# Start addresses of the float32r operand tiles moved onto multiples of 256 bytes

## The chip, the cores and the metric

The kernel runs on one core of one Trainium2 chip. The metric is the device time of one execution in microseconds (us), as the median of three runs. Beside the runs there is one profiled execution; all rows below come from it.

## What is computed

The reference is a decoder trunk of two layers over 256 tokens of width 1024, in float32.

```python
for i in range(2):
    h = rmsnorm(x, norm_mix[i]); memn = rmsnorm(mem, norm_mem[i])
    if i == 0: mix, q = s5_mixer(p[..., :768], ...), p[..., 768:]          # p = h @ w_in_a
    else:      mix, q = rwkv7_mixer(p[..., :2560], ...), p[..., 2560:]     # p = h @ w_in_b
    x = x + concat([mix, memory_cross_attn(q, memn, w_kv_mem[i])]) @ w_out[i]
    h2 = rmsnorm(x, norm_ffn[i])
    x = x + (swiglu(h2, ...) if i == 0 else moe_swiglu(h2, ...))           # dense, then 2 of 8 experts
return rmsnorm(x, norm_final)
```

Each of the 8 experts has a gate and an up matrix of 1024 x 3584 and a down matrix of 3584 x 1024.

## The kernel before

**Products.** Large products are made in float32r from operands split in two: a tile of weights `w` (2 MB, one DMA on SP's queue, `wload`, L63) is cut into 4 parts by `split` (L168 to 184). ScalarE writes the rounded part `wsh` (L182), VectorE the rest `wsl = w - wsh` (L183). Activations come as a pair as well (`xeh`/`xel`, `ath`/`atl`, `hTh`/`hTl`, `aTh`/`aTl`, `cath`/`catl`). `mm3` (L186) then issues three matmuls into one accumulator:

```python
TE.matmul(ps, xp[0], wh, ...)   # L188
TE.matmul(ps, xp[0], wl, ...)   # L189
TE.matmul(ps, xp[1], wh, ...)   # L190
```

The second argument is the operand that is loaded into the array (128 x 128, the row LDWEIGHTS of engine PEld); the third streams through it, 512 columns at a time. A profile row names the streaming operand first: `gu<-wsh,xeh`.

**Stages.** S5 mixer, memory attention and the first output projection (0 to 200 us), the dense SwiGLU ("FFN" below, to about 390 us), RWKV-7 (to 565 us), the second output projection and the router (to 615 us), and the expert layer (615 to 1615 us). The expert layer walks 8 experts x 7 chunks of 512 hidden columns, 56 jobs. A job has 24 matmuls for gate, 24 for up (both write `gu`, the loaded operand is `xe`) and 24 for down (accumulators `yac`, the loaded operand is `at`, the transposed activation of the job before), and four transposes against `ident` (L1646). Down matmuls of one job stand between gate and up matmuls of the next. Fetching an expert's tokens (`Gather`: `Gm` loaded, `xhp` streaming, L1448) comes in chunk 3 of the expert before; adding its result back (`combine`, L1681 and L1682) comes between gate and up of chunk 1 of the expert after. Weights pass through a ring of seven 2 MB tiles, the parts `wsh` and `wsl` through four buffers each.

**Addresses.** Tiles come from pools that are stacked in SBUF, some from the low end, some (`side="right"`) from the high end. `pad(pool, n)` takes n bytes. Even experts keep `Gm`, `xe`, `GT` and the small tile `wsl` of row weights (L1473; another tile than the split's `wsl`) in pool `mp0`, odd experts in `mp1`, which lies elsewhere. `smk` makes a small tile in the pool `sml` (two buffers a name).

Of the kernel before, what the change touches and what calls it, by code (L numbers as in the profile page):

```python
# [9 lines left out]
F32 = mybir.dt.float32  # L10
# [7 lines left out]
P = 128  # L18
# [31 lines left out]
def build(ctx, tc, a, out, taps=None):  # L50
    nc = tc.nc
    taps = taps or {}
    V, S, G, TE = nc.vector, nc.scalar, nc.gpsimd, nc.tensor
# [5 lines left out]
    def pool(st, name, bufs, **kw):  # L59
        return st.enter_context(tc.tile_pool(name=name, bufs=bufs, reuse_waits="tile", **kw))  # L60
# [4 lines left out]
    def pad(pl, n):  # L65

        pl.tile([P, n // 4], F32, name="pad", tag="pad")

    x, mem = a["x"][0], a["mem"][0]
    consts = pool(ctx, "consts", 1)  # L70
    sml = pool(ctx, "sml", 2)
    mhalf = consts.tile([P, 1], F32, name="mhalf")
    V.memset(mhalf, -0.5)
# [3 lines left out]
    keep = pool(keep_st, "keep", 1, side="right")  # L77
# [72 lines left out]
    def smk(shape, dt, name):  # L150
        return sml.tile(shape, dt, name=name)
# [10 lines left out]
    def mkpair(pl, shape, name, bufs=None):  # L162

        kw = {} if bufs is None else {"bufs": bufs}
        return (pl.tile(shape, F32R, name=name + "h", tag=name + "h", **kw),
                pl.tile(shape, F32R, name=name + "l", tag=name + "l", **kw))
# [140 lines left out]
    with ExitStack() as st:  # L307
# [6 lines left out]
        def mm():  # L314
            return pp.tile([P, 512], F32, name="mm", tag="mm", bufs=2)

        def tr():
            return pp.tile([P, 4, P], F32, name="trp", tag="tr", bufs=2)
# [4 lines left out]
        def bup():  # L323
            return pp.tile([P, 2, 4, P], F32, name="bu", tag="bu", bufs=1)
# [45 lines left out]
        t = mm()  # L370
# [122 lines left out]
        for ri, sg in ((0, 1.0), (1, -1.0)):  # L493
            t = tr()
# [62 lines left out]
        t = bup().rearrange("p a b t -> p (a b t)")  # L557
# [13 lines left out]
        for i in range(0, NST, 2):  # L571
            t = tr()
# [68 lines left out]
                yield  # L641

        cat0 = mkpair(keep, [P, KD, T], "cat")
        pad(keep, 96)


        sw = pool(st, "s5w", 1)
# [68 lines left out]
        for q in range(QC):  # L716
            Yn = front(q + 1) if q + 1 < QC else None
            for _ in range(NFILL):
                next(fill, None)
            back(q, Y)  # L720
            Y = Yn
# [713 lines left out]
    class Gather:  # L1435
# [27 lines left out]
        def back(self, tr):  # L1463

            self.GT = self.mp.tile([P, NH, P], F32R, name="GT")
            t, e = tr(), self.e
            for h in range(NH):
                TE.transpose(t[:, h, :], self.Gm[:, h, :].bitcast(F32), ident)
            for h in range(NH):
                TE.matmul(t[:, 2, 0:2], self.Gm[:, h, :].bitcast(F32), wt[:, h, e, :], start=h == 0, stop=h == NH - 1,  # L1470
                          skip_group_check=True)
            S.copy(self.GT, t[:, 0:2, :])
            wsl = self.mp.tile([P, 32], F32, name="wsl")  # L1473
            V.tensor_copy(wsl[:, 0:2], t[:, 2, 0:2])
            self.w, self.rs = wsl[:, 0:1], wsl[:, 1:2]

    with ExitStack() as st:
# [304 lines left out]
```

## Time and profile before

| | |
|---|---|
| median of 3 runs | 1628.95 us (1626.86 to 1629.56) |
| the profiled execution's own time | 1630.18 us |
| its span, first to last instruction | 1628.4 us |
| TensorE matmul busy (PE) | 1538.1 us, 94% |
| VectorE busy (DVE) | 1321.5 us, 81% |
| ScalarE busy (ACT) | 1061.3 us, 65% |
| granted TensorE clock, mean | 0.97 of full speed |
| moved by DMA | 423.44 MB |

Matmuls overlap in the records: the next one starts before the last one has ended, so a busy PE says only that there was no gap. How fast matmuls go is read from start to start. The expert layer is 1000 of the 1628 us.

### The profile page before, as it was taken

The numbers are of one execution on the slowest core, as the hardware profiler recorded it, in microseconds if no ns is written. First come the engines' busy times: TensorE is split into PE (matmuls) and PEld (weight loads), VectorE is DVE, ScalarE is ACT, GpSimd is POOL, SyncE is SP. The second block draws the span as 40 slices with busy tenths as digits, with TensorE's granted clock in tenths as the row PEclk, the third lists the DMA queues.
The fourth block names the chain that finished last, engine by engine and source line by source line (L and its number), as shares of the span: only waits on it lengthen the run. The fifth ranks groups of instructions, "written<-read, shape, count | busy, mean of one in ns | idle before, by whom it ended". The sixth has DMA issues, their size and how long they took to land. (4 is left out here: it accounts for less than half of the span.)

```text
span 1628.4 us, 20876 instructions
## 1 busy us (share of the span) xinstructions
PE 1538.1 (94%) x7973; PEld 1283.0 (79%) x7973; DVE 1321.5 (81%) x1566; ACT 1061.3 (65%) x1362; POOL 196.6 (12%) x222
## 2 busy tenths in 40 slices
PE   5888999998979989999999999999999999999996
PEld 4667788887968868888888888888888887888885
DVE  7996655545797567899899899899899898888986
ACT  3534654434734336777777777777777777777774
POOL 5756000003464230000000000000000000000000
PEclk9789999999998988999999999999999999999998
DMA  6210755532320677999999999999999999999970
GB/s 165 67 52 32 279 203 181 182 129 81 111 65 21 222 270 261 337 371 351 337 376 350 343 363 358 337 369 360 341 360 362 361 339 359 356 339 354 355 273 28
DMA packets 198835, 423.44 MB, mean 260 GB/s; under 512 B 14772, under 2 KB 36422, under 8 KB 198726
## 3 DMA queue, kind: packets, MB, share of 16 engines
q1 hardware_dynamic: 196554, 419.34, 70.9%
q10 hardware_dynamic: 2172, 2.68, 0.6%
q8 instruction: 64, 1.05, 0.3%
q14 instruction: 45, 0.37, 0.1%
HBM read 420.96 MB, written 1.05 MB: 259 GB/s over the span
## 5 line engine op out<-in xcount | busy, mean ns | idle before, releaser
L183 DVE TENSOR_TENSOR wsl<-w,wsh 128x1024 fp32r<-128x1024 f32 (+1 forms) x757 | 896.6, 1217 | 158.1 <-ACT wsh L182 150.4
L182 ACT CAST wsh<-w 128x1024 fp32r<-128x1024 f32 (+1 forms) x757 | 782.4, 1045 | 260.4 <-PE gu L190 108.2
L189 PE MATMUL gu<-wsl,xeh 128*128 128x512 f32 x896 | 353.4, 394 | 0.0
L188 PE MATMUL gu<-wsh,xeh 128*128 128x512 f32 x896 | 351.5, 399 | 1.5 <-DVE xs L1686 1.5
L190 PE MATMUL gu<-wsh,xel 128*128 128x512 f32 x896 | 352.5, 393 | 0.0
L188 PEld LDWEIGHTS gu<-wsh,xeh 128*128 128x128 f32 x896 | 169.2, 189 | 38.7 <-ACT wsh L182 2.3
L190 PEld LDWEIGHTS gu<-wsh,xel 128*128 128x128 f32 x896 | 169.1, 189 | 37.2 <-DVE xel L1461 0.2
L189 PEld LDWEIGHTS gu<-wsl,xeh 128*128 128x128 f32 x896 | 169.2, 189 | 36.8
L189 PE MATMUL yac<-wsl,ath 128*128 128x512 f32 x440 | 174.8, 397 | 0.0
L190 PE MATMUL yac<-wsh,atl 128*128 128x512 f32 x440 | 173.8, 395 | 0.0
L276 POOL TENSOR_TENSOR rs<-vv,mhalf 128x1 f32<-128x1 f32 x8 | 4.4, 554 | 1223.4 <-DVE vv L275 1223.4
L188 PE MATMUL yac<-wsh,ath 128*128 128x512 f32 x440 | 138.9, 397 | 0.0
L190 PEld LDWEIGHTS yac<-wsh,atl 128*128 128x128 f32 x440 | 83.0, 189 | 19.0
L188 PEld LDWEIGHTS yac<-wsh,ath 128*128 128x128 f32 x440 | 82.5, 188 | 18.5
L189 PEld LDWEIGHTS yac<-wsl,ath 128*128 128x128 f32 x440 | 83.2, 189 | 16.8
L189 PE MATMUL mm<-wsl,hTh 128*128 128x512 f32 (+1 forms) x192 | 71.1, 372 | 0.0
L188 PE MATMUL mm<-wsh,hTh 128*128 128x512 f32 (+1 forms) x192 | 71.1, 374 | 0.0
L190 PE MATMUL mm<-wsh,hTl 128*128 128x512 f32 (+1 forms) x192 | 70.3, 373 | 0.0
L1648 ACT CAST ath<-t 128x512 fp32r<-128x512 f32 x55 | 32.2, 586 | 31.6 <-PE yac L189 30.6
L1640 DVE TENSOR_TENSOR sg<-sg,gu 128x512 f32<-128x512 f32 x56 | 38.2, 683 | 14.4 <-PE gu L190 14.4
L190 PE MATMUL dn<-hTh,wsC 128*128 128x256 f32 x160 | 46.6, 291 | 1.0 <-POOL wsC L1138 0.9
L188 PE MATMUL dn<-hTh,wsC 128*128 128x256 f32 x160 | 46.2, 289 | 0.0
(530 smaller groups left out, 2142.7 us busy)
## 6 DMA issues: line engine op xcount, KB each, us to landing
w<-in_moe_w_gate_dram SPq DMA_DIRECT2D x55, 2048.0 KB, 8.1
w<-in_moe_w_up_dram SPq DMA_DIRECT2D x55, 2048.0 KB, 7.9
w<-in_moe_w_down_dram SPq DMA_DIRECT2D x54, 2048.0 KB, 9.0
w<-in_w_in_b_dram SPq DMA_DIRECT2D x22, 512.0 KB, 3.4
w<-in_ffn_w_gate_dram SPq DMA_DIRECT2D x5, 2048.0 KB, 7.8
w<-in_ffn_w_up_dram SPq DMA_DIRECT2D x5, 2048.0 KB
w<-in_ffn_w_down_dram SPq DMA_DIRECT2D x5, 2048.0 KB, 7.8
w<-in_w_out_dram SPq DMA_DIRECT2D x4, 2048.0 KB
```

Source lines behind the costliest of these rows:

```text
L182: S.copy(hv, src)
L183: (eng or V).tensor_sub(lv, src, hv.bitcast(F32))
L188: TE.matmul(ps, xp[0], wh, start=start, stop=False, skip_group_check=True)
L189: TE.matmul(ps, xp[0], wl, start=False, stop=False, skip_group_check=True)
L190: TE.matmul(ps, xp[1], wh, start=False, stop=stop, skip_group_check=True)
L276: hold.append(G.tensor_tensor(rs, vv, mhalf, op=OP.pow).ins)
L1640: V.tensor_mul(sg, sg, ps[1])
L1648: S.copy(at[0], t)
```

## The change

Three edits. A pad of 64 bytes opens the pool `consts`. The pad behind `cat0` in the pool `keep` grows from 96 to 224 bytes. The 128-byte tile `wsl` of row weights leaves `mp0` and `mp1`; it becomes an 8-byte tile of `sml`.

```diff
     consts = pool(ctx, "consts", 1)
+    pad(consts, 64)
     sml = pool(ctx, "sml", 2)
...
         cat0 = mkpair(keep, [P, KD, T], "cat")
-        pad(keep, 96)
+        pad(keep, 224)
...
             S.copy(self.GT, t[:, 0:2, :])
-            wsl = self.mp.tile([P, 32], F32, name="wsl")
-            V.tensor_copy(wsl[:, 0:2], t[:, 2, 0:2])
+            wsl = smk([P, 2], F32, "wsl")
+            V.tensor_copy(wsl, t[:, 2, 0:2])
             self.w, self.rs = wsl[:, 0:1], wsl[:, 1:2]
```

In the built programs the instructions are the same and stand in the same order on every engine. `consts` moves by 64 bytes; behind `sml`, which has two 32-byte slots more, the tiles stacked from the low end move up by 128 bytes. Those stacked from the high end behind `keep` move down by 128. Behind `mp0` the two effects cancel, so the split's buffers of the expert layer and `mp1` stay. Start addresses of the operands, modulo 256:

```
tiles (role)                                             before  after
wsh, wsl of the expert layer and of output projection 2     0      0   streaming
xeh, xel, Gm, GT of odd experts (mp1)                       0      0   loaded
xeh, xel, Gm, GT of even experts (mp0)                    128      0   loaded
ath, atl (down, all experts)                              128      0   loaded
cath, catl (output projections)                           128      0   loaded
xhp (gather), ye (combine)                                128      0   streaming
hTh, hTl, aTh, aTl (FFN, RWKV)                            128      0   loaded
wsh, wsl of output projection 1 and FFN; wsC of RWKV      128      0   streaming
w (target of the weight DMAs, read by the split)          128      0
ident (streams in transposes)                             160    224   streaming
sg, xr, ye as input of transposes                         128      0   loaded
```

## Rows read from the trace of the kernel before

**Rows 1.** Windows: us, busy us (x instructions) of each engine, PEclk, DMA share, GB/s.

```profile
200.00:360.00 160.00, 160.00 (x777) 135.01 (x776) 86.62 (x94) 75.62 (x94) 0.56 (x1) 1.00 0.50 178
640.00:1600.00 960.00, 958.46 (x4318) 784.19 (x4317) 868.33 (x830) 750.31 (x806) 0.00 (x0) 1.00 0.94 346
```

**Rows 2.** Waits, 640 to 1600 us: engine line <- waited for: us in total, times, longest.

```profile
ACT wsh L182 <- PE gu L190: 102.1, 260, 0.8
...
ACT wsh L182 <- PE yac L190: 59.2, 156, 0.9
...
PEld gu L188 <- ACT wsh L182: 2.3, 2, 1.2
```

**Rows 3.** Timeline of PE, even expert 2: start us, us, engine line op.

```profile
896.25 0.40 PE L189 MATMUL gu<-wsl,xeh 128*128 128x512 f32 x1
...
907.17 0.64 PE L188 MATMUL yac<-wsh,ath 128*128 128x512 f32 x2
```

**Rows 4.** Timeline of PE, odd expert 3.

```profile
1021.42 0.39 PE L189 MATMUL gu<-wsl,xeh 128*128 128x512 f32 x1
...
1032.08 0.64 PE L188 MATMUL yac<-wsh,ath 128*128 128x512 f32 x2
```

**Rows 5.** Timeline of PE, a run of down matmuls and what follows it.

```profile
890.45 0.39 PE L189 MATMUL yac<-wsl,ath 128*128 128x512 f32 x1
...
894.65 0.60 PE L1646 MATMUL t<-ident,sg 128*128 128x128 f32 x4
```

**Rows 6.** Timeline of PE, a run of FFN matmuls and what follows it.

```profile
250.22 0.39 PE L190 MATMUL mm<-wsh,hTl 128*128 128x512 f32 x1
...
271.54 0.27 PE L768 MATMUL trp<-ident,sgl 128*128 128x128 f32 x1
```

**Rows 7.** Timeline of PE, gather for an odd, then for an even expert.

```profile
917.85 0.40 PE L1448 MATMUL gu<-xhph,Gm 128*128 128x512 f32 x1
...
919.71 0.40 PE L189 MATMUL gu<-wsl,xeh 128*128 128x512 f32 x1
...
1042.63 0.39 PE L1448 MATMUL gu<-xhph,Gm 128*128 128x512 f32 x1
...
1044.45 0.39 PE L189 MATMUL gu<-wsl,xeh 128*128 128x512 f32 x1
```

**Rows 8.** Timeline of PE, first combine matmul after experts 1, 2 and 3.

```profile
879.99 0.39 PE L1681 MATMUL gu<-yeh,GT 128*128 128x512 f32 x1
...
1005.17 0.39 PE L1681 MATMUL gu<-yeh,GT 128*128 128x512 f32 x1
...
1129.33 0.39 PE L1681 MATMUL gu<-yeh,GT 128*128 128x512 f32 x1
```

**Rows 9.** Groups of DVE, FFN, then expert layer: busy, mean ns | idle before.

```profile
L183 DVE TENSOR_TENSOR wsl<-w,wsh 128x1024 fp32r<-128x1024 f32 x54 | 65.7, 1224 | 60.3 <-ACT wsh L182 60.2
...
L183 DVE TENSOR_TENSOR wsl<-w,wsh 128x1024 fp32r<-128x1024 f32 x649 | 770.5, 1223 | 69.6 <-ACT wsh L182 62.1
```

**Rows 10.** Transposes on PE: line, count: duration ns min/median/max, first and last start.

```profile
L574 PE MATMUL trp<-ident,BC x48: 272/328/477, 41.4 to 58.3; 128*128 128x128 f32 x48
L768 PE MATMUL trp<-ident,sgl x44: 271/273/277, 226.2 to 323.7; 128*128 128x128 f32 x44
```

**Rows 11.** SP's queue, 640 to 1560 us: its wait; an issue, KB, us to landing.

```profile
SPq L63 <- DVE wsl L183: 849.6, 155, 8.5
...
w<-in_moe_w_gate_dram SPq DMA_DIRECT2D x51, 2048.0 KB, 8.1
```

**Rows 12.** Timeline of PE after a wait, output projection 2.

```profile
569.50 0.88 PE L1362 MATMUL rw<-ident,ysq 128*128 128x128 f32 x3 [4.07 <-DVE ysq L1359]
570.03 0.77 PE L188 MATMUL mm<-wsh,cath 128*128 128x512 f32 x1
...
574.45 0.55 PE L189 MATMUL mm<-wsl,cath 128*128 128x512 f32 x1
```

**Rows 13.** Timeline of PEld in the combine of expert 5.

```profile
1383.46 0.19 PEld L188 LDWEIGHTS gu<-wsh,xeh 128*128 128x128 f32 x1 [1.17 <-ACT wsh L182]
```

## The prediction

> **What bounds the kernel now.** I read the windows first, then the waits, then single matmuls. From 640 to 1600 us TensorE has a matmul in flight for 958.46 of 960.00 us at the granted clock 1.00, while VectorE is busy for 868.33 and ScalarE for 750.31 [rows 1]. The waits say who paces whom: ScalarE's cast, the first step of the split, waits for TensorE to give a `wsh` buffer back, 102.1 us behind gate and up and 59.2 behind down, while TensorE's longest wait of this kind comes to 2.3 us in all [rows 2]. So the expert layer goes at the pace of its matmuls, and the pace is the thing to look at, from start to start.
>
> There the trace holds an experiment already made. Even experts keep their loaded operand at 128 modulo 256 and stream weights from 0; odd experts load from 0 and stream from 0. In even expert 2, 47 gate and up matmuls in a row take from 896.25 to 907.17 us, 232.3 ns each [rows 3]. In odd expert 3 the same 47 take from 1021.42 to 1032.08, 226.8 ns each [rows 4]. Same line, same shape, same clock: 5.5 ns apart. Down, whose loaded `at` lies at 128 in every expert, takes 4.20 us for 18 matmuls, 233.3 ns [rows 5].
>
> Two more groups tell what it hangs on. The FFN loads from 128 and streams from 128, and goes at 226.8 ns (94 matmuls in 21.32 us) [rows 6], so a loaded operand at 128 costs nothing by itself. That stage moves half as much by DMA and has an idler VectorE [rows 1], so one could blame its quiet. The gather answers that inside the expert layer: it streams `xhp` from 128, and there the sides change places. For an odd expert (`Gm` at 0) its 8 matmuls take 1.86 us, 232.5 ns; for an even one (`Gm` at 128) 1.82 us, 227.5 ns [rows 7]. What costs 5 ns is a loaded and a streaming operand that differ in their start modulo 256. The forecast hardly needs this reading, since after the change all these pairs are 0 and 0, the very pair of rows 4.
>
> **The change part by part.** *Gate and up of the even experts* go from 128/0 to 0/0: 4 experts x 7 jobs x 48 = 1344 matmuls x 5.5 ns = 7.4 us. *Down of all experts* goes from 128/0 to 0/0: 56 x 24 = 1344 matmuls. Its own row would give 233.3 - 226.8 = 6.5 ns, but its run also has matmuls that follow another accumulator, so I take the 5.5 ns of the clean pair again: 7.4 us. Bounds for both: 5.0 ns (rows 7) to 6.5. *Output projection 2*, 96 matmuls at 128/0: 0.5 us at full pace, but ten of them run at half clock [rows 12] and it waits for splits in between; between 0 and 0.5, I take 0.3. *Gather of the odd experts*: 4 x 0.04 = 0.2 us. *Combine* of the odd experts, 32 matmuls at 0/128: 0 to 0.2, I take 0.
>
> On the other side stands *what no longer matches*. `ident` goes from 160 to 224 and the inputs of the transposes from 128 to 0, so the 288 transposes of the expert layer that had both starts in the upper half of 256 bytes now have one in each. The nearest rows: L574 streams `ident` at 160 over tiles at 32, L768 over tiles at 128, and their shortest records are 272 and 271 ns [rows 10]. That gives 0.3 us; the far bound is the whole 5.5 ns each, 1.6 us. I take 0.3 lost.
>
> *What costs nothing.* The split reads and writes other addresses, but VectorE's part takes 1224 ns in the FFN (all three tiles at 128) and 1223 in the expert layer (source at 128, results at 0) [rows 9]; with all at 0 I see no reason for a third number. FFN, RWKV and output projection 1 go from 128/128 to 0/0, between which rows 6 and 4 show no difference (226.8 and 226.8). The row weights are written and read by the same instructions from another place; two buffers in `sml` repeat what `mp0` and `mp1` gave, and their reader, the combine of expert e, is done before the gather of expert e + 2 writes. No instruction changes its place, so no queue is passed.
>
> Sum: 7.4 + 7.4 + 0.3 + 0.2 - 0.3 = 15.0 us of matmul time.
>
> *How much reaches the end.* From combine to combine the trace gives 125.18 us for the stretch with 11 of the 14 half-steps (24 gate or up matmuls each) in even expert 2, and 124.16 for odd expert 3 [rows 8]: 1.02 apart. By the count it should be (11 - 3) x 24 x 5.5 ns = 1.06 plus 0.04 for the gather, 1.10. So 93% of the difference arrives, and 15.0 becomes 14.0. Nothing stands behind to take it back: after the last expert come a norm and the output. The profiled execution would go from 1630.18 to 1616.2; the median of the runs lies 1.2 lower, 1628.95, and goes to **1615.0 us**.
>
> **The rivals.** *Everything streams as before.* The trace could mislead, if the even and odd pools differed in something besides the start, or if the build did not place the tiles so. The addresses are read from the built program, and the sign of the gather, turned round by its own operand, speaks against the first. Time: 1628.95.
> A page of the Trainium skill speaks for this rival: "SBUF — State Buffer" (A bandwidth-pool intuition that's wrong) gives the loading of weights a second, independent read port beside that of the streaming operand, by which no matmul could depend on the two starts together and the sum would be 0. The trace disagrees: 232.3 against 226.8 ns [rows 3, 4].
>
> *The split falls behind.* VectorE is busy 90.5% of the expert layer; if TensorE needs 14 us less it is 868 of 946, 92%. That is room on the mean, not in the jobs with a combine, where VectorE has six more operations. There TensorE has waited already: 1.17 us for `wsh` in the combine of expert 5 [rows 13] and once more like it, near 1509 us, but in no combine before. A wait of 0.9 us at six more places takes 5.6 us of the gain back: 14.0 - 5.6 = 8.4, 1620.5. For it: these two waits. Against: odd experts run two thirds of each job at 0/0 already, and no wait follows them. With it goes the DMA: its share would rise from 0.94 to 0.95, but SP's queue spends 849.6 of 920 us waiting for a free buffer, and a tile lands 8.1 us after its issue, where six other tiles of the ring (168 tiles in 1000 us, 6 us each) are used up first, in 36 [rows 1, 11]. So I don't make it a case of its own.
>
> *Slower: the granted clock falls.* If such waits grow longer, TensorE may be granted the lower of its two levels, 1.2 instead of 2.4 GHz, behind each. After a wait of 4.07 us ten matmuls took from 570.03 to 574.45, 4.42 us instead of 2.32 [rows 12]: 2.1 us a time. The gain is gone from the seventh such stretch on, and the kernel is slower by over 0.2% from the ninth; with one at each of 15 gathers and combines it is 1628.95 - 14.0 + 31.5 = 1646. Against it: the waits of rows 13 are a quarter as long and the clock stayed at 1.00 throughout [rows 1].
>
> **How the numbers follow.** About 0.2% (3.3 us) is what a measurement of this kernel can tell from no change. Forecast, 1615.0: 0.82; its own range is 1612.3 (6.5 ns on down, all of it arriving) to 1618 (5.0 ns, 93%, the transposes at their far bound: 6.7 + 6.7 + 0.5 - 1.6 = 12.3, 11.4 arriving, 1617.5). Split behind, 1618 to 1624: 0.09. As before: 0.06. Slower: 0.03. The range must leave out no more than 0.2, so from 1612 to 1621 it holds the forecast and the nearer part of the second case. Faster 0.91, same 0.06, slower 0.03.
>
> **What would show it.** In the changed kernel's trace 47 gate and up matmuls of expert 2 should take 10.66 us as those of expert 3 do, 18 down matmuls 4.1, the gathers 1.82 for both kinds. Stretches from combine to combine should be equal in even and odd experts, near 123 us. VectorE's split should stay at 1223 ns and the transposes within 2 ns. It would be wrong if the pace falls to 227 and the stretches don't shorten (then TensorE's waits name who took it), or if the pace of even experts stays at 232 (then the start modulo 256 is not what they differ in).

## The result and the profile after

The change makes the kernel faster, by 0.8%: a median of 1615.47 us (20 runs, 1613.57 to 1629.16 but for one of 2819.01) against 1628.61 for the kernel before beside it (20 runs, 1626.64 to 1647.07). The ratio is 0.9919, 95% interval 0.9894 to 0.9944. The forecast was 1615.0. The profiled execution after took 1614.67 us, its span is 1612.9. The run of 2819.01 us, at a mean granted clock of 0.80, has no profile, is not explained and is left out of the ratio. Some executions of most kernels, of the one before too, take up to some 20 us more than the rest; where one of them has a profile, the granted clock is low for 14 or 41 us in the RWKV stage. So kernels are compared below by stretches of the expert layer, and the last experiments are about that stage.

Line numbers after are one higher than before. In all fences of a timeline the columns are start us, us, engine, line, operation, operands, with the idle time before it in brackets. TensorE, kernel after: gate and up of even expert 2, then of odd expert 3, 47 matmuls each between the rows shown (those of [rows 3, 4]).

```profile
891.05 0.39 PE L190 MATMUL gu<-wsl,xeh 128*128 128x512 f32 x1
...
901.71 0.61 PE L189 MATMUL yac<-wsh,ath 128*128 128x512 f32 x2
...
1014.03 0.39 PE L190 MATMUL gu<-wsl,xeh 128*128 128x512 f32 x1
...
1024.68 0.61 PE L189 MATMUL yac<-wsh,ath 128*128 128x512 f32 x2
```

10.66 us and 10.65: 226.8 ns a matmul for the even expert, which took 232.3, and 226.6 for the odd one, which stays (a row is exact to 0.01 us, 0.2 ns over 47 matmuls and 0.6 over 18). The same timeline, 18 down matmuls [rows 5]:

```profile
885.37 0.39 PE L190 MATMUL yac<-wsl,ath 128*128 128x512 f32 x1
...
889.46 0.27 PE L1647 MATMUL t<-ident,sg 128*128 128x128 f32 x1
```

4.09 us, 227.2 ns, where it was 233.3. The gathers [rows 7], for an odd and then for an even expert, 8 matmuls each:

```profile
912.16 0.39 PE L1449 MATMUL gu<-xhph,Gm 128*128 128x512 f32 x1
...
913.97 0.39 PE L190 MATMUL gu<-wsl,xeh 128*128 128x512 f32 x1
...
1035.13 0.39 PE L1449 MATMUL gu<-xhph,Gm 128*128 128x512 f32 x1
...
1036.94 0.39 PE L190 MATMUL gu<-wsl,xeh 128*128 128x512 f32 x1
```

Both take 1.81 us; they were 1.86 and 1.82. The first combine matmul after experts 1, 2 and 3 [rows 8]:

```profile
874.94 0.39 PE L1682 MATMUL gu<-yeh,GT 128*128 128x512 f32 x1
...
997.97 0.39 PE L1682 MATMUL gu<-yeh,GT 128*128 128x512 f32 x1
...
1120.94 0.39 PE L1682 MATMUL gu<-yeh,GT 128*128 128x512 f32 x1
```

The stretches are 123.03 and 122.97 us, where they were 125.18 and 124.16. Even and odd experts are now alike. Behind the pace stands what the windows and the waits (640 to 1600 us), the DVE group (640 to 1580 us) and the transposes of the expert layer show, to be read beside the rows of before [rows 1, 2, 9, 10]:

```profile
640.00:1600.00 960.00, 957.82 (x4370) 790.76 (x4369) 874.58 (x840) 756.61 (x813) 0.00 (x0) 1.00 0.93 345
```

```profile
ACT wsh L183 <- PE gu L191: 91.5, 243, 0.8
...
ACT wsh L183 <- PE yac L191: 46.5, 134, 0.9
...
PEld gu L189 <- ACT wsh L183: 2.4, 2, 1.2
```

```profile
L184 DVE TENSOR_TENSOR wsl<-w,wsh 128x1024 fp32r<-128x1024 f32 x644 | 762.0, 1221 | 60.4 <-ACT wsh L183 49.6
```

```profile
L1647 PE MATMUL t<-ident,sg x224: 270/272/308, 631.9 to 1590.4; 128*128 128x128 f32 x112
```

In the same 960 us TensorE now starts 4370 recorded matmuls instead of 4318 and is as full as before. It still paces: ScalarE's cast waits 91.5 + 46.5 = 138.0 us for it (161.3 before), TensorE waits 2.4 us (2.3). The split takes 1221 ns (1223). The transposes, whose two starts both lay in the upper half of 256 bytes and no longer do, take 272 ns in the median, as before.

Stage by stage, us from the first matmul of one stage to the first of the next (the last combine and the norm count as the tail, to the end of the span):

```
                                            before     after
start to output projection 1                167.38    166.46
output projection 1                          22.51     22.35
FFN                                         189.50    189.44
FFN to RWKV                                   9.45      9.46
RWKV                                        181.19    181.24
output projection 2 and router               45.36     45.02
expert layer, to the last combine           997.41    983.95
tail                                         15.57     15.03
```

Of the 15.4 us between the two spans 13.46 lie in the expert layer and 0.34 in output projection 2. The 0.9 at the start and the 0.5 of the tail don't count for the change: the other kernels of this study, the unimproved ones too, needed 165.06 to 166.89 and 14.93 to 15.36 there.

### The profile page after: what moved, and what is told of

It reads as the page before. It is cut to its first block, busy times and chain, and to the rows that moved or that the text cites. A ratio compares the mean times of both kernels' runs of the same rounds, so it can differ in the third digit from the quotient of the medians.

```text
span 1612.9 us, 20876 instructions
## 1 busy us (share of the span) xinstructions
PE 1522.6 (94%) x7973; PEld 1278.7 (79%) x7973; DVE 1319.4 (82%) x1566; ACT 1062.0 (66%) x1362; POOL 196.8 (12%) x222
## 5 line engine op out<-in xcount | busy, mean ns | idle before, releaser
L1641 DVE TENSOR_TENSOR sg<-sg,gu 128x512 f32<-128x512 f32 x56 | 38.2, 681 | 13.7 <-PE gu L191 13.7
L191 PE MATMUL dn<-hTh,wsC 128*128 128x256 f32 x160 | 46.5, 291 | 1.0 <-POOL wsC L1139 0.9
```

The source lines that it names most:

```text
L191: TE.matmul(ps, xp[1], wh, start=False, stop=stop, skip_group_check=True)
L1641: V.tensor_mul(sg, sg, ps[1])
```

## The experiments

**Theories.** *Matching*: a matmul takes some 5 ns more where its loaded and its streaming operand start at different places modulo 256. *Alignment*: operands must start on a multiple of 256, as the change puts them. *The row weights*: their move to `sml` is what counts, by less traffic or another place. Stretches from combine to combine, in us, even and odd experts in turn, and the expert layer as a whole:

```
expert                1       2       3       4       5       6    layer
before             124.18  125.18  124.16  125.12  124.20  126.08   997.4
after              122.99  123.03  122.97  122.98  123.01  123.78   984.0
all at 128         123.05  123.03  123.05  123.05  123.03  123.80   984.2
row weights alone  123.03  123.00  122.99  122.98  123.05  123.80   982.5
pads alone         124.17  125.12  124.18  125.12  124.17  126.08   997.5
down at 128        123.85  123.86  123.85  123.89  123.95  124.89   991.3
even at 128        123.46  124.53  123.59  124.51  123.57  125.38   992.3
offsets a          125.76  125.43  125.76  125.44  125.54  126.26  1004.5
offsets b          125.88  126.04  125.89  126.04  125.92  127.00  1008.1
```

**All at 128.** From before; the row-weight tile grows by 128 bytes, by which every operand of the expert layer starts at 128 modulo 256.

```diff
-            wsl = self.mp.tile([P, 32], F32, name="wsl")
+            wsl = self.mp.tile([P, 64], F32, name="wsl")
```

> The kernel before, with the row-weight tile of each expert pool 128 bytes larger, so that in the expert layer every operand of the float32r products starts at 128 modulo 256, loaded and streaming alike. Nothing starts at a multiple of 256. Theory (only the difference of the two starts counts): gate and up of even and odd experts and down at 227 ns from start to start, like the changed kernel, so about 1615.5 us (1613 to 1618). Rival (each start has to be a multiple of 256): the odd experts lose their 227 ns too, all 4032 matmuls at 232 ns or more, 1628.6 + 1344 x 5.5 ns = 1636 us.

TensorE's timeline, first combine matmul after experts 1 to 3:

```profile
894.92 0.39 PE L1681 MATMUL gu<-yeh,GT 128*128 128x512 f32 x1
...
1017.95 0.39 PE L1681 MATMUL gu<-yeh,GT 128*128 128x512 f32 x1
...
1140.99 0.39 PE L1681 MATMUL gu<-yeh,GT 128*128 128x512 f32 x1
```

123.03 and 123.04 us, as after, with no operand of the large products on a multiple of 256 and the row weights where they were. Alignment falls, and so does the worth of the row weights' move; matching stands. The median, 1623.23 us (5 runs, 1614.92 to 1634.83; ratio 0.9943, 0.9904 to 0.9982), is spread by the RWKV stage, which took 201.42 us in the profile.

**The row weights alone.** From before; the third edit without the pads. Everything in the expert layer starts at 192, loaded and streaming.

```diff
-            wsl = self.mp.tile([P, 32], F32, name="wsl")
-            V.tensor_copy(wsl[:, 0:2], t[:, 2, 0:2])
+            wsl = smk([P, 2], F32, "wsl")
+            V.tensor_copy(wsl, t[:, 2, 0:2])
```

> The kernel before with the move of the row weights alone, both pads as before. All operands of the expert layer then start at 192 modulo 256. Theory (difference): expert layer at 227 ns throughout, 13.5 us gained there; in the FFN the loaded hT stays at 128 while the weights stream from 192, a difference of 64, for which no row exists: 0 to 5.5 ns x 480 matmuls, 0 to 2.6 us lost, and 0 to 1.0 in the output projections; 1615.5 to 1619. Rival (multiples of 256): no gain, 1636 us as in the run with all at 128.

The expert layer goes at 227.2 ns, mean of all back-to-back 512-column matmuls, and takes 982.5 us. The FFN here loads from 128 and streams from 192. Its timeline, 94 matmuls [rows 6]:

```profile
226.70 0.40 PE L190 MATMUL mm<-wsh,hTl 128*128 128x512 f32 x1
...
248.23 0.38 PE L768 MATMUL trp<-ident,sgl 128*128 128x128 f32 x2
```

21.53 us, 229.0 ns instead of 226.8. The pace of the expert layer follows from matching; that a difference of 64 costs only 2 ns does not. Yet the median is 1631.78 us (10 runs, 1615.93 to 1635.75; ratio 0.9989, 0.9952 to 1.0025), where 1615.5 to 1619 was expected: 15 us won in one stage and no gain in sum. This is taken up below.

**The pads alone.** The changed kernel with the row weights back in `mp0` and `mp1`.

```diff
-            wsl = smk([P, 2], F32, "wsl")
-            V.tensor_copy(wsl, t[:, 2, 0:2])
+            wsl = self.mp.tile([P, 32], F32, name="wsl")
+            V.tensor_copy(wsl[:, 0:2], t[:, 2, 0:2])
```

> The changed kernel without the move of the row weights, both pads kept. In the expert layer the weights then stream from 64, even experts load from 192, odd ones from 64, down loads from 192; in the FFN hT loads from 0 and the weights stream from 192. Theory: even experts and down at a difference of 128, 232 ns, odd ones 227, as in the kernel before: no gain there, and 0 to 2.6 us lost in the FFN: 1628 to 1632 us. Rival (multiples of 256): 232 everywhere, 1636 us or more. If the move of the row weights had a worth of its own (another pool, a wait less), the stretches would differ from those before by more than 0.2 us.

Weights stream from 64 here; even experts and down load from 192, odd experts from 64. The stretches are those of before within 0.1 us, the median 1630.84 (10 runs, 1628.72 to 1636.74; ratio 1.0005, 0.9987 to 1.0023). Neither the pads nor the move of the row weights is worth anything but for the addresses: with the one alone the starts in the expert layer agree, with the other alone they don't.

**Down at 128, even experts at 128.** Each undoes one of the two large terms in the changed kernel.

```diff
     mp = pool(moe, "mp", 2)
+    pad(mp, 64)
```

> The changed kernel with one thing undone: the pool of the down operand, at, moved by 128 bytes, so that down is at 128/0 again in all experts (ye of the combine too). Theory: 1344 matmuls x 5.5 ns come back, of which 93 to 100% reach the end, 6.9 to 7.4 us: 1622.5 us; stretches from combine to combine 0.9 us longer in even and odd experts alike; gate and up stay at 227. Rival (the two changed groups overlap in what they free, so that one of them gives the whole gain): 1615.5 or 1628.6.

```diff
     mps = [pool(moe, "mp0", 1)]
+    pad(mps[0], 128)
...
+            if self.mp is mps[0]:
+                self.mp.tile([P, 32], F32, name="tail", tag="tail")
```

> The changed kernel with another thing undone: the pool of the even experts moved by 128 bytes (and closed by 128 more, so that nothing behind it moves against the rest), so that gate and up of even experts are at 128/0 again. Theory: 6.9 to 7.4 us come back, 1622.5 us; stretches of even experts 1.9 x (11/14) = 1.5 us longer, those of odd experts 0.4; together with the run on down the two parts sum to the whole gain. Rival: as in that run, 1615.5 or 1628.6.

The combine rows of the first, then of the second:

```profile
875.67 0.40 PE L1683 MATMUL gu<-yeh,GT 128*128 128x512 f32 x1
...
999.53 0.40 PE L1683 MATMUL gu<-yeh,GT 128*128 128x512 f32 x1
```

```profile
876.94 0.39 PE L1685 MATMUL gu<-yeh,GT 128*128 128x512 f32 x1
...
1001.47 0.40 PE L1685 MATMUL gu<-yeh,GT 128*128 128x512 f32 x1
...
1125.06 0.40 PE L1685 MATMUL gu<-yeh,GT 128*128 128x512 f32 x1
```

With down at 128 the stretches are 123.85 to 123.95, even and odd alike (the last one 124.89); with even experts at 128 they are 124.53 and 123.59 for experts 2 and 3. The layer is 7.4 us longer with the one and 8.4 with the other, medians 1622.38 (10 runs; ratio 0.995, 0.991 to 0.999) and 1623.02 (10 runs; 0.9971, 0.9927 to 1.0015). Together that is 15.8, more than the 13.5 of the whole, to which they were expected to sum.

**A third variant of this kind: only `xel` at 128.** In the changed kernel a tile of 128 bytes stands between `xeh` and `xel` in `mp0`, another of 128 at its end.

```diff
-            self.xe = mkpair(self.mp, [P, KD, P], "xe")
+            xeh = self.mp.tile([P, KD, P], F32R, name="xeh", tag="xeh")
+            if self.mp is mps[0]:
+                self.mp.tile([P, 32], F32, name="mid", tag="mid")
+            self.xe = xeh, self.mp.tile([P, KD, P], F32R, name="xel", tag="xel")
...
+            if self.mp is mps[0]:
+                self.mp.tile([P, 32], F32, name="tail", tag="tail")
```

> The changed kernel with one of the two loaded tiles of the even experts apart: xeh stays at 0, xel starts at 128, so that in gate and up every third matmul loads an operand that differs from the stream (the program issues wsl-xeh, wsh-xel, wsh-xeh in turn). It asks which matmul pays. If a matmul pays for its own loaded operand: the interval behind wsh-xel is 232 ns, the two others 227. If it pays while the next operand is loaded beside its stream: the interval behind wsl-xeh, in which xel is loaded, is 232, the others 227. If a change of the start between loads costs: both. Time 1615.5 + 448 x 5.5 ns = 1618 us by the first two, 1620 by the third.

One matmul in three has different starts. Gate and up of expert 2, 47 matmuls:

```profile
893.16 0.40 PE L190 MATMUL gu<-wsl,xeh 128*128 128x512 f32 x1
...
904.03 0.62 PE L189 MATMUL yac<-wsh,ath 128*128 128x512 f32 x2
```

231.3 ns, not a third of the way but four fifths; 1621.08 us (1 run). Sorted by what a matmul is, over all even experts, the mean to the next start is 233.6 ns for those on `xel` themselves (409), 232.4 for those on `wsl` and `xeh` during which `xel` is loaded for the next (438), and 228.3 for those with neither (399). So it is the third expectation, both. One reading is that a matmul pays when its own loaded operand differs and also when the next one's does, once, not twice; that it pays for the change of the start between two loads as well fits this run too.
The 2.3 us that the two half-undone kernels cost beyond the whole lie in part at the seams between matching and differing work, of which they have more than before. With down at 128, gate and up, whose own starts agree, take 0.95 us more than in the changed kernel, and they take it at the head of a run, behind down: the first three matmuls go at 231.5, 230.2 and 229.6 ns (228.9, 228.1 and 228.0 in the changed kernel), those from the tenth on at 226.7 in both. Where the rest of the 2.3 us lies was not worked out.

**Other offsets.** In the changed kernel, even experts, odd experts and down are put at 32, 64 and 192 (a), then at 96, 160 and 224 (b), while weights stream from 0. The edit is that of a; b has 96, [P, 40], 160 and 32 in the four places.

```diff
     mps = [pool(moe, "mp0", 1)]
+    pad(mps[0], 32)
...
+            if self.mp is mps[0]:
+                self.mp.tile([P, 56], F32, name="tail", tag="tail")
...
+    pad(mps[1], 64)
     mp = pool(moe, "mp", 2)
+    pad(mp, 64)
```

> The changed kernel with loaded operands at other distances from the streaming weights (at 0): even experts' xe at 32, odd experts' xe at 64, at of down at 192. Theory as it stands (any difference modulo 256 costs 5 ns): 232 ns in all three. Variant (only the half of 256 bytes in which a start lies counts, 0 to 127 or 128 to 255): 227, 227, 232. Variant (the cost grows with the distance): below 232 for 32, 64 and 192 alike, with 64 and 192 equal. Rival (multiples of 256 wanted): 232 or more everywhere. A pace below 226.8 anywhere would point to a better kernel. Time 1622 to 1629 us by the first two, some 1618 by the third.

> As the run with 32, 64 and 192, at the remaining distances: even experts' xe at 96, odd experts' xe at 160, at of down at 224. Theory as it stands (any difference): 232 ns in all three. Variant (the half of 256 bytes): 227, 232, 232. Variant (growing with the distance): 96 and 160 equal and near 231, 224 near 228. Rival (multiples of 256): 232 or more everywhere.

Variant a, gate and up of expert 2 and of expert 3:

```profile
896.91 0.39 PE L190 MATMUL gu<-wsl,xeh 128*128 128x512 f32 x1
...
907.86 0.39 PE L189 MATMUL yac<-wsh,ath 128*128 128x512 f32 x1
...
1022.41 0.39 PE L190 MATMUL gu<-wsl,xeh 128*128 128x512 f32 x1
...
1033.38 0.40 PE L189 MATMUL yac<-wsh,ath 128*128 128x512 f32 x1
```

233.0 and 233.4 ns; in variant b 11.00 and 10.96 us, 234.0 and 233.2. Down goes at 230.8 ns in a (a difference of 64) and at 233.2 in b (32). 1635.37 and 1639.55 us (1 run each), the expert layer 7 and 11 us longer than before: above the 1622 to 1629 that was expected, since all 4032 matmuls of the three products pay, and only a difference of 64 costs less than the whole. No offset goes below 226.8 ns, so there was nothing more to win this way.

**`keep` at 96.** The changed kernel with the pad behind `cat0` as before: the FFN loads from 128 and streams from 0.

```diff
-        pad(keep, 224)
+        pad(keep, 96)
```

> The changed kernel with the larger pad in the pool keep undone, so that tiles stacked from the high end stay at 128: in the FFN hT loads from 128 while the weights stream from 0, and cat in both output projections as well; the expert layer is untouched. Theory: FFN gate and up at 232 ns where the changed kernel and the kernel before have 227: 480 x 5.5 ns + 96 half-wide x 2.7 ns = 2.9 us lost there and up to 1.0 in the output projections, 1618.4 to 1619.4 us; expert layer as in the changed kernel. Rival (FFN doesn't care, because VectorE and DMA are half idle there): 1615.5.

FFN, 94 matmuls:

```profile
227.84 0.40 PE L191 MATMUL mm<-wsh,hTl 128*128 128x512 f32 x1
...
249.77 0.49 PE L769 MATMUL trp<-ident,sgl 128*128 128x128 f32 x3
```

21.93 us, 233.3 ns, with the idler VectorE and the half DMA share of this stage: the cost is not one of the expert layer. The FFN takes 192.14 us (189.44), 2.7 more where 2.9 was expected; output projection 1 takes 24.11 (22.35; 21.89 to 23.35 in the other kernels whose starts agree there); the expert layer stays at 983.3. By the stages that is 4.5 us more than the changed kernel, by the medians 3.1: 1618.58 us (5 runs, 1616.22 to 1624.09; ratio 0.9915, 0.9888 to 0.9942).

**Where the gain of the row weights alone went.** The same kernel again, to see whether its median holds:

> The kernel before with the move of the row weights alone, a second time. In its first runs the expert layer took as long as in the changed kernel, but the median was 1631.8 us, with the granted clock lower in most executions, behind the waits of the RWKV stage near 505 us. If that was chance: a median of 1616 to 1620. If the other starts of the RWKV tiles (192 from the low end, 128 from the high end) bring the clock down: again above 1630.

It does: 1630.51 us (10 runs, 1619.16 to 1633.69; ratio 0.9969, 0.9931 to 1.0007). In the two series 12 of 20 executions took 1629.9 us or more. The windows of this kernel around 500 us (us, busy us of PE, PEld, DVE, ACT, POOL, granted clock, DMA share, GB/s):

```profile
490.02:493.00 2.98, 2.98 (x7) 2.44 (x8) 2.91 (x6) 1.41 (x3) 2.45 (x3) 0.50 0.00 0
493.50:500.00 6.50, 6.50 (x49) 6.05 (x47) 6.16 (x11) 3.59 (x7) 5.08 (x5) 1.00 0.00 0
505.50:545.00 39.50, 39.50 (x344) 34.35 (x338) 14.42 (x25) 10.89 (x29) 9.52 (x7) 0.50 0.07 21
```

TensorE is busy all the time, but for 39.5 us at a granted clock of 0.50, 1.2 instead of 2.4 GHz. The timeline of all engines just before, in this kernel:

```profile
490.02 6.26 PE L1218 MATMUL rw<-A,Kt 128*128 128x256 f32 x20 [13.01 <-ACT Vc L1205]
...
497.61 3.43 POOL L1292 TENSOR_TENSOR mxk<-mxr,mxk 128x1536 f32<-128x1536 f32 x1
497.74 3.34 DVE L1061 TENSOR_TENSOR tmp<-NB,X 128x31 f32<-128x31 f32 x1
...
501.34 1.98 DVE L1065 STREAM_TRANSPOSE X<-X 128x1024 f32<-128x1024 f32 x1
...
503.37 1.83 PE L1084 MATMUL iv<-X,Nt 32*32 32x32 f32 x68 [3.20 <-DVE X L1065]
```

And in the profiled execution of before:

```profile
491.25 7.04 PE L1218 MATMUL rw<-A,Kt 128*128 128x256 f32 x20 [13.00 <-ACT Vc L1205]
...
498.25 0.54 DVE L1061 TENSOR_TENSOR tmp<-NB,X 128x31 f32<-128x31 f32 x1
498.82 0.19 DVE L1063 TENSOR_TENSOR X<-X,tmp 128x31 f32<-128x31 f32 x1
...
499.05 2.15 DVE L1065 STREAM_TRANSPOSE X<-X 128x1024 f32<-128x1024 f32 x1
...
499.58 3.46 POOL L1292 TENSOR_TENSOR mxk<-mxr,mxk 128x1536 f32<-128x1536 f32 x1
...
502.12 1.71 PE L1084 MATMUL iv<-X,Nt 32*32 32x32 f32 x96
```

Read from the top. After a wait of 13 us TensorE goes at the low clock; in the first profile full clock is back within 3.5 us, in the second after 5.0. So the 20 matmuls take 6.26 us in the one and 7.04 in the other, GpSimd is sooner done with the masks that it makes from them, and its 3.4 us product of `mxk` starts before VectorE has ended its chain on `X` rather than 0.57 us after it. A VectorE step that begins behind it takes 3.34 us instead of 0.54 and ends with it (501.08 against 501.04). TensorE waits 3.20 us for `X`, and the low clock follows. The same pattern stands in all four profiles of this study with a long low stretch behind this place (20 matmuls in 6.12 to 6.29 us, one VectorE step of 3.34 or 3.37, a wait of 3.19 to 3.48, then 13.7 or 41 us at 0.50), and in none of the other eight up to here (6.91 to 7.53 us, no wait for `X` of 1 us).
The Trainium skill, "SBUF — State Buffer" (Who interferes with whom; Summary: rules for kernel authors), has VectorE and GpSimd share a pair of ports as an exclusive lock, by which a VectorE operation with two SBUF inputs, issued while a GpSimd operation reads SBUF, stands still until that ends. The rows agree: 3.34 instead of 0.54 us for the step with two inputs, while the transpose of `X` (L1065), with one input, takes 2.15 us beside the product and 1.98 without it.

**The collision taken away.** The product gets a small forerunner on GpSimd that reads a column of `X`, so that it starts behind VectorE's last step. Once on the row weights alone, once on the changed kernel.

```diff
         with tc.issue_after(box["mask"].ins):
+            done = G.tensor_copy(vb[:, 1, 0, 0:1], X[:, 31, 0:1])
+        with tc.issue_after(done.ins):
             G.tensor_mul(k2, r_, k2)
```

> The kernel before with the row-weight move alone (as the third and the last run so far), and one thing more: GpSimd's product of mxk in the RWKV stage first reads one column of X, so that it starts behind the last step of VectorE's inverse; two GpSimd instructions stand where one stood, nothing else is moved. What the profiles show: in the four with the half-clock stretch of 14 or 41 us from 504 us on, GpSimd's 3.4 us product starts before VectorE is done with X, one VectorE step that starts behind it takes 3.3 us instead of 0.5 or 0.2, TensorE waits 3.2 to 3.5 us for X, and then the clock is down; in the others the product starts 0.6 us after the last step. Theory, the collision starts it: with the collision taken away no wait of 3 us for X is left, no half-clock stretch follows it, and the median falls from 1631 to about 1616 (before less 13.5 of the expert layer, and up to 1 us more for the FFN at 229 ns), none or one of ten executions at 1629 or above. Rival, the clock falls there for its own reasons and the wait goes with it: 12 of 20 executions without this edit were at 1630 or above, so 5 to 7 of ten again, median 1630.

Timeline of all engines:

```profile
491.29 6.31 PE L1218 MATMUL rw<-A,Kt 128*128 128x256 f32 x20 [12.99 <-ACT Vc L1205]
...
499.25 0.19 DVE L1063 TENSOR_TENSOR X<-X,tmp 128x31 f32<-128x31 f32 x1
...
499.51 0.19 POOL L1292 COPY KB<-X 128x1 f32<-128x1 f32 x1 [0.59 <-DVE X L1063]
499.66 3.47 POOL L1294 TENSOR_TENSOR mxk<-mxr,mxk 128x1536 f32<-128x1536 f32 x1
...
501.67 1.71 PE L1084 MATMUL iv<-X,Nt 32*32 32x32 f32 x96 [0.18 <-DVE X L1065]
```

This execution had the early return of the clock (6.31 us), the one that led to the collision in four others. GpSimd was free at 498.92 us, before VectorE's last step at 499.25, and now waits 0.59 us for it; VectorE's steps take 0.19, TensorE waits 0.18 us, and from 504 to 545 us the mean granted clock is 0.92 (0.50 in the profile with the collision, 0.96 in that of before). The median is 1616.11 us (6 runs, 1614.06 to 1618.59; ratio 0.992, 0.9901 to 0.994), against 1631.78 and 1630.51 without the edit: none of 6 runs above 1619, where 12 of 20 had been at 1629.9 or more. So the rows show the collision gone and the long low stretch with it, and the medians show the gain back; all ten profiles without the collision are without the stretch. One doubt stays: the runs with and without the edit were made on three chips, and the kernel before, run beside them, had 7 of 26 and 2 of 13 executions above 1640 us on the two without the edit and none of 11 on the one with it. A part of the difference in medians may be the chip's.

> The changed kernel with the same one addition: GpSimd's product of mxk reads one column of X first. Theory, the collision starts the half-clock stretch: the median stays at 1615.5 (the addition costs at most the 0.2 us of a small GpSimd instruction, in a place where GpSimd had 0.6 us to spare against VectorE), and the 3 of 20 executions at 1627 to 1629 go: ten of ten under 1621. Rival, the clock falls for its own reasons: one or two of ten at 1627 or above, median as before; with so few the run beside it decides. If the addition costs something that the profile does not show, the median rises to 1617 or more.

1614.93 us (6 runs, 1613.26 to 1622.54; ratio 0.9916, 0.9892 to 0.9941), not to be told from the changed kernel by the median. None of 6 was at 1626 or above, where 3 of the changed kernel's 20 were at 1626.9 to 1629.2; so few runs do not show that these are gone, and one of the six, 1622.54, lies above the 1621 under which all were expected. In its profile the full clock came back late (20 matmuls in 7.07 us) and there was nothing to avoid.

## Why the prediction was right

- *The pace.* Even gate and up were to go from 232.3 to 226.8 ns and did, to the digit. Down was given 5.5 ns a matmul against the 6.5 that its own run showed; the run gained 6.1 (233.3 to 227.2). Taking the clean pair was on the low side for this run, but too high for the sum: 2688 matmuls and 13.46 us make 5.0 ns each.
- *What it hangs on.* The reading that the two starts must agree was not needed for the number, but it is what the experiments bear out: 128 and 128, 192 and 192, 64 and 64 (odd experts of the pads alone), and 0 and 0 all go at 227 ns. The Trainium skill, "SBUF — State Buffer" (A bandwidth-pool intuition that's wrong), gives the loading of weights an independent second read port. If that is taken to mean that the two starts together can't matter, the runs disagree, with 227 ns where they agree and 229 to 234 where they don't.
- *The 93% that arrive.* The four terms of the expert layer (7.4 + 7.4 + 0.2 - 0.3) times 0.93 give 13.7; measured 13.46. The product was right, its two factors were not. All of the matmul time arrives; it is the price that was too high. Over the whole layer, back-to-back gate and up matmuls of even experts go from 232.3 to 227.1 ns and those of down from 232.5 to 227.7, and 1344 x 5.26 + 1344 x 4.78 ns is 13.5 us, the whole of what was measured; TensorE's waits did not change (2.3 and 2.4 us). The 5.5 ns of the two clean runs was a price for long runs of gate and up. In down the first matmuls of a run go slower with starts that agree as well (230.5 and 229.6 ns for the second and third after the change, 226.8 from the tenth on). That the 0.93, read from whole stretches, made up for a price read from the best ones is luck in part.
- *Output projection 2.* 0.3 forecast, 0.34 measured. The match says little, since this stage with the router took 43.95 to 45.22 us in the other kernels; its back-to-back matmuls went from 232.3 to 228.7 ns. *The gather* 0.05 us a time, forecast 0.04.
- *The transposes.* 0.3 us was set against the gain for them, because both starts lay in the upper half of 256 bytes. By the prediction's own rule, the start modulo 256, they never agreed: 160 and 128 before, 224 and 0 after. The pair that agrees stands in offsets b (224 and 224; `L1652` is the line there):

```profile
L1652 PE MATMUL t<-ident,sg x224: 270/272/308, 632.9 to 1615.0; 128*128 128x128 f32 x112
```

  The median is 272 ns in all three, and from start to start they take 109 ns in all three. Nothing was lost, and the far bound of 1.6 us was idle.
- *What costs nothing.* FFN 189.50 to 189.44 us, RWKV 181.19 to 181.24, the split 1223 to 1221 ns: as said.
- *Rival, everything as before*: fell with the pace. *Rival, the split falls behind*: TensorE's waits did not grow, and the stretch behind the combine of expert 5 [rows 13] keeps its extra time, 0.8 us after (123.78 against 123.0) and 0.9 before (126.08 against 125.15). (Its sum is a little off: six waits of 0.9 us make 5.4 us, not 5.6.) *Rival, the granted clock falls*: not at the gathers and combines, where it stays at 1.00. But it named the right mechanism at the wrong place: in the RWKV stage a wait of 3.2 to 3.5 us on another engine is followed by 14 or 41 us at half clock, which makes that stage 7 or 20 us longer. The executions of before at 1644 to 1647 us fit that, though none of them has a profile. With other addresses, those of the row weights alone, it took the whole gain of the expert layer away. The forecast did not look there, since the profile of before, read alone, shows no such wait. That the changed kernel's addresses let most of its executions escape it was not foreseen: there the median was lucky.

## What to carry to other kernels

Compare the mean interval from start to start of matmuls of one shape in different places of one kernel; where they differ, list the start addresses of both operands before looking for contention. Where loaded and streaming operands of float32r matmuls agree modulo 256 a matmul gave 227 ns here, else 229 to 234, and which residue it is did not matter (0, 64, 128 and 192 were run). Judge such a change by the stage it touches, and look at the spread of the runs as well: a race between two engines elsewhere can hide a gain from the median, and with one ordering edge there it was back.

## What the runs showed of the hardware that was not expected

The price by the difference of the starts (streaming less loaded, modulo 256), mean from start to start over the 512-column float32r matmuls of the stage named (for 64 the range of FFN and down), at the granted clock 1.00:

```
difference     0    32    64          96     128    160    192    224
ns           227   233   229 to 231   233    232    234    233    233
```

It is a matter of agreeing or not, save at 64, where about half is paid; it does not grow with the distance, and half of 256 is no exception. No larger modulus counts: in the kernel before, `hTh` and the FFN's `wsh` start 896 and 640 bytes past a multiple of 1024, 256 apart, and go at 226.8 ns. Differences that are no multiple of 32 were not run. The 128-column transposes of float32 tiles don't show the price (272 ns at differences of 0, 32 and 224). Which part of the chip makes the two operands meet is not known from these runs.

The targets of the weight DMAs moved from 128 to 0 modulo 256 with the change. Packets of 2048 bytes take 84 ns in the median and those of 4096 bytes 159 ns both before and after; their start in SBUF didn't matter.

An engine that gets its full clock back earlier can end later: 0.8 us won by TensorE in 20 matmuls at 490 us let GpSimd and VectorE collide and cost 7 us (two profiles) or 20 us (two). Why the clock returns after 3 us in some executions and after 5 in others, and why it did so more often with the row weights alone, stays open.
